# RMSNorm with swish: 32-row groups per partition for loads and stores, and a small transfer ahead of gamma's

## The chip, the cores and the metric

The kernel runs on one core of a Trainium2 chip. The metric is the device time of an execution in microseconds (us); the kernel before has a median of 160.43 us over 12 runs (160.1 to 160.9). A profile is one execution recorded by the hardware profiler. Its span runs from the first to the last recorded work of the program, and the device time is a little longer. The names in it: DVE is VectorE, ACT is ScalarE, POOL is GpSimd, SP is SyncE, whose only work here is to issue loads and to wait. "ACTq" and "SPq" are the sequencers that issue transfers. TensorE has no work in this kernel.

## The reference

The input is 16 x 1024 rows of 512 float32 values; every row is treated alone.

```python
rms = np.sqrt(np.mean(x ** 2, axis=-1, keepdims=True) + eps)
x_norm = x / rms * gamma
return (x_norm * (1.0 / (1.0 + np.exp(-x_norm)))).astype(np.float32)
```

That is 33.55 MB in and 33.55 MB out. A row is 2 KB.

## The kernel before

**Tiles.** The 16384 rows are cut into eleven tiles, one after the other in HBM. Tile `t` takes `sizes[t]` rows for each of the 128 partitions: 4, 4, 8, then six times 16, then 8 and 8, which makes 128 rows per partition. Within a tile, partition p holds consecutive rows, so for a tile of 16 rows each partition moves one contiguous piece of 32 KB, and the whole tile is contiguous in HBM. The buffer `xb` has room for 96 rows per partition and is used as a ring: tile 0 to 7 fill it once, tiles 8, 9 and 10 use the places of tiles 0 to 3 again. Everything happens in place: rows are loaded into `xb`, normalised there, passed through swish there and stored from there.

**Chunks.** The work goes by chunks of 4 rows per partition, 32 in all. For chunk k:

- `square(k)` on ScalarE: the fourth row is squared with its sum accumulated (L159), the other three are squared into a PSUM buffer (L166). Before the first chunk of a tile, ScalarE waits for the tile's load.
- `sums(k)` on VectorE (L204): the three sums of squares from PSUM.
- GpSimd adds eps (L141) and takes the power -0.5 (L148).
- `norm(k)` on VectorE (L215): four instructions, one for each row, multiply by the reciprocal root and by gamma.
- `swish(k)` on ScalarE (L178), over all four rows.

**Order.** The order on each engine is written out by hand. VectorE runs sums(k) and then norm(k-1). ScalarE runs square(k), then any store that is due, then swish(k-2). A store of a tile (L183) is issued from ScalarE's queue two chunks after the tile's last chunk number, so that it does not hold up the queue; it waits for the last swish of its tile. The PSUM buffer exists twice, so square(k) also waits for sums(k-2).

**Transfers.** Loads are issued by SP in order (L118), as early as the ring lets them: tiles 0 and 1 even ahead of the program's starting barrier, tiles 2 to 7 right after it; tile 8 waits for the stores of tiles 0, 1 and 2, tile 9 for that of tile 3 (L116). Gamma is loaded from ScalarE's queue into four partitions (L187) after GpSimd has zeroed the buffer (L136), and VectorE spreads it over the partitions (L228). At the end SP waits for all stores (L238).

Of the kernel before, what the change touches and what calls it, by code (L numbers as in the profile page):

```python
# [8 lines left out]
@with_exitstack  # L9
def kernel(  # L10
    ctx: ExitStack,
    tc: tile.TileContext,
    x: bass.AP,
    gamma: bass.AP,
    eps: bass.AP,
    out: bass.AP,
):
    nc = tc.nc
    P = nc.NUM_PARTITIONS
    AF = mybir.ActivationFunctionType  # L20
    ALU = mybir.AluOpType
    fp32 = mybir.dt.float32
    bf16 = mybir.dt.bfloat16

    xf = x.flatten_outer_dims()
    of = out.flatten_outer_dims()
    R, D = xf.shape


    sizes = [4, 4, 8] + [16] * 6 + [8, 8]  # L30
    ring = 96
    early = 2
    cn = 4
    n_sq = 3
    N = sum(sizes)
    assert N * P == R, (N, R)


    tiles = []
    done = 0  # L40
    for sz in sizes:
        assert done % ring + sz <= ring
        tiles.append((done * P, sz, done % ring))
        done += sz
    T = len(tiles)

    chunks = [
        (t, r, r == at)
        for t, (_, sz, at) in enumerate(tiles)
        for r in range(at, at + sz, cn)  # L50
    ]
    K = len(chunks)
    ends = []
    e = 0
    for sz in sizes:
        e += sz // cn
        ends.append(e)

    inv_d = 1.0 / float(D)
    eps_f = float(eps)  # L60

    tc.close()
    tc.compile()  # L65

    def sbuf(name, shape, dt=fp32):
        return nc.alloc_sbuf_tensor(name, shape, dt).ap()

    xb = sbuf("xb", [P, ring, D])  # L70
    gamma4 = sbuf("gamma4", [P, D])
    gamma_sb = sbuf("gamma_sb", [P, D])
    junk = [sbuf(f"junk{i}", [P, D], bf16) for i in range(2)]
    neg_half = sbuf("neg_half", [P, cn])
    ms = sbuf("ms", [P, K, cn])
    aeps = sbuf("aeps", [P, K, cn])
    rstd = sbuf("rstd", [P, K, cn])
    sq = [nc.alloc_psum_tensor(f"sq{i}", [P, 4, D], fp32).ap() for i in range(2)]

    ld = [nc.alloc_semaphore(f"ld{t}") for t in range(T)]  # L80
    st = [nc.alloc_semaphore(f"st{t}") for t in range(T)]
    s_gld = nc.alloc_semaphore("s_gld")
    s_zero = nc.alloc_semaphore("s_zero")
    s_half = nc.alloc_semaphore("s_half")
    s_gamma = nc.alloc_semaphore("s_gamma")
    s_acc = nc.alloc_semaphore("s_acc")
    s_sq = nc.alloc_semaphore("s_sq")
    s_sum = nc.alloc_semaphore("s_sum")
    s_eps = nc.alloc_semaphore("s_eps")
    s_rstd = nc.alloc_semaphore("s_rstd")  # L90
    s_norm = nc.alloc_semaphore("s_norm")
    s_swish = nc.alloc_semaphore("s_swish")

    def need(ins, sem, value):
        return ins.wait_op(sem, value, "sem-ge")

    def dram(ap, t):
        first, sz, _ = tiles[t]
        return ap[first : first + P * sz].rearrange("(p n) d -> p n d", n=sz)

    def buf(t):
        _, sz, at = tiles[t]
        return xb[:, at : at + sz, :]


    stored_by_sync = set()

    def load(t):
        _, sz, at = tiles[t]
        waits = [  # L110
            u for u in range(t)
            if tiles[u][2] < at + sz and at < tiles[u][2] + tiles[u][1]
            and u not in stored_by_sync
        ]
        for u in waits:
            nc.sync.wait_ge(st[u], 16)  # L116
            stored_by_sync.add(u)
        return nc.sync.dma_start(out=buf(t), in_=dram(xf, t)).then_inc(ld[t], 16)  # L118

    entry = nc.main_func.blocks[0].instructions  # L120
    here = nc.cur_bb.bb.instructions
    for t in range(early):
        ins = load(t).ins
        assert here[-1] is ins or here[-1].name == ins.name
        here.pop()
        at = next(
            i for i, other in enumerate(entry)
            if other.engine == mybir.EngineType.SP
            and isinstance(other, mybir.InstDrain)
        )  # L130
        entry.insert(at, ins)
    for t in range(early, T):
        load(t)


    nc.gpsimd.memset(gamma4, 0.0).then_inc(s_zero, 1)  # L136
    nc.gpsimd.memset(neg_half, -0.5).then_inc(s_half, 1)  # L137
    nc.gpsimd.wait_ge(s_half, 1)
    for k in range(K):
        need(  # L140
            nc.gpsimd.tensor_scalar(  # L141
                out=aeps[:, k, :], in0=ms[:, k, :], scalar1=eps_f, scalar2=None,
                op0=ALU.add,
            ),
            s_sum, k + 1,
        ).then_inc(s_eps, 1)
        need(
            nc.gpsimd.tensor_tensor(  # L148
                out=rstd[:, k, :], in0=aeps[:, k, :], in1=neg_half, op=ALU.pow
            ),  # L150
            s_eps, k + 1,
        ).then_inc(s_rstd, 1)


    def square(k):
        t, at, first = chunks[k]
        if first:
            nc.scalar.wait_ge(ld[t], 16)  # L158
        acc = nc.scalar.activation(  # L159
            out=junk[k % 2], in_=xb[:, at + n_sq, :], func=AF.Square,  # L160
            scale=inv_d**0.5, accum_out=ms[:, k, n_sq : n_sq + 1],
        )
        if k >= 2:
            need(acc, s_acc, k - 1)
        acc.then_inc(s_acc, 1)
        square = nc.scalar.activation(  # L166
            out=sq[k % 2][:, 0:n_sq, :], in_=xb[:, at : at + n_sq, :],
            func=AF.Square, scale=inv_d**0.5,
        )
        if k >= 2:  # L170
            need(square, s_sum, k - 1)
        square.then_inc(s_sq, 1)

    def swish(k):
        _, at, _ = chunks[k]
        rows = xb[:, at : at + cn, :]
        need(
            nc.scalar.activation(out=rows, in_=rows, func=AF.Silu), s_norm, k + 1  # L178
        ).then_inc(s_swish, 1)

    def store(t):
        need(
            nc.scalar.dma_start(out=dram(of, t), in_=buf(t)), s_swish, ends[t]  # L183
        ).then_inc(st[t], 16)

    need(
        nc.scalar.dma_start(out=gamma4[0:P:32, :], in_=gamma.partition_broadcast(4)),  # L187
        s_zero, 1,
    ).then_inc(s_gld, 16)
    nc.scalar.preload_act_table_set("silu_and_others")  # L190
    stored = 0
    for k in range(K + 3):
        if k < K:
            square(k)
        while stored < T and ends[stored] <= k - 2:
            store(stored)
            stored += 1
        if 2 <= k < K + 2:
            swish(k - 2)


    def sums(k):
        need(
            nc.vector.tensor_reduce(  # L204
                out=ms[:, k, 0:n_sq], in_=sq[k % 2][:, 0:n_sq, :], op=ALU.add,
                axis=mybir.AxisListType.X,
            ),
            s_sq, k + 1,
        ).then_inc(s_sum, 1)

    def norm(k):
        _, at, _ = chunks[k]
        for j in range(cn):
            row = xb[:, at + j, :]
            ins = nc.vector.scalar_tensor_tensor(  # L215
                out=row, in0=row, scalar=rstd[:, k, j : j + 1], in1=gamma_sb,
                op0=ALU.mult, op1=ALU.mult,
            )
            if j == 0:
                need(ins, s_rstd, k + 1)  # L220
        ins.then_inc(s_norm, 1)

    for k in range(K + 1):
        if k < K:
            sums(k)
        if k == 0:
            need(
                nc.vector.stream_shuffle(gamma_sb, gamma4, [0] * 32), s_gld, 16  # L228
            ).then_inc(s_gamma, 1)
        if k == 1:  # L230
            nc.vector.wait_ge(s_gamma, 1)
        if k >= 1:
            norm(k - 1)


    for t in range(T):
        if t not in stored_by_sync:
            nc.sync.wait_ge(st[t], 16)  # L238

# [34 lines left out]
```

## Time and profile before

| what | value |
|---|---|
| median of 12 runs | 160.43 us (160.1 to 160.9) |
| the profiled execution's own time | 160.66 us |
| its span | 159.3 us |
| VectorE busy | 139.1 us, 87% of the span |
| ScalarE busy | 125.1 us, 79% |
| GpSimd busy | 83.4 us, 52% |
| moved by DMA | 67.14 MB, 421 GB/s over the span |
| DMA queues | q1 (SP, loads) 33.56 MB, q10 (ScalarE, stores and gamma) 33.56 MB |
| norm (L215) | 128 instructions, 87.7 us, 755 ns each |
| sums (L204) | 32 instructions, 56.4 us, 1761 ns each |
| swish (L178) | 32 instructions, 61.1 us, 1908 ns each |
| square into PSUM (L166) | 32 instructions, 45.9 us, 1433 ns each |

Times in a profile are counted from the span's start. The page shows the busy share of each engine in 40 equal slices, one digit for each in tenths; the row "DMA" is the mean of the 16 DMA engines. The chain is followed back from the last instruction: at every step to what released it. A row of the list of waits names who waited, for whom, the total, how often, and the longest. In the DMA view a queue's row has its packets, its megabytes and the share of the 16 engines' time.

### The profile page before, as it was taken

Reading aid. Unit: us, or ns where it says so; the run is one execution under the profiler, and the core shown is the slowest. Engines: PE = TensorE matmul, PEld = TensorE weight load, DVE = VectorE, ACT = ScalarE, POOL = GpSimd, SP = SyncE. Lnnn points to the kernel's source line nnn. Section 1 sums busy time; section 2 is a strip of 40 time slices with the busy share of each in tenths; the row PEclk is TensorE's granted clock in tenths of the full one; section 3 lists DMA queues with packets and bytes.
Section 4 is the critical chain, followed back from the end, with each engine's and each line's share of the span. In section 5 each row is a group of like instructions: output and inputs, shape, how many; then the busy total and the mean of one; then the engine's idle time right before and its main releaser. Section 6 shows DMA issues by size and latency. Waiting matters only on the chain.

```text
span 159.3 us, 437 instructions
## 1 busy us (share of the span) xinstructions
DVE 139.1 (87%) x162; ACT 125.1 (79%) x129; POOL 83.4 (52%) x70
## 2 busy tenths in 40 slices
DVE  0298977999999999999999999999999999996600
ACT  1939849888888889988888888888998888883410
POOL 1043552444455555444444445888888888889000
DMA  6999999989989999999999999899999999999995
GB/s 251 434 502 395 395 389 450 477 360 479 477 360 452 399 469 413 403 477 436 395 438 477 395 411 494 382 457 407 477 391 424 440 461 411 420 485 395 403 444 230
DMA packets 3179, 67.14 MB, mean 421 GB/s; under 512 B 356, under 2 KB 356, under 8 KB 360
## 3 DMA queue, kind: packets, MB, share of 16 engines
q1 hardware_dynamic: 1584, 33.56, 49.6%
q10 hardware_dynamic: 1592, 33.56, 49.0%
q14 instruction: 3, 0.02, 0.0%
HBM read 33.56 MB, written 33.55 MB: 421 GB/s over the span
## 4 chain that ended last, share of the span: by engine, by line
DVE 76%; DMA 13%; ACT 2%; POOL 2%; issue 0%; SPq 0%; ACTq 0%
DVE xb L215 47%; DVE ms L204 29%; DMA xb<-in_x_dram 13%; POOL aeps L141 2%; ACT xb L178 1%; ACT sq L166 1%; POOL rstd L148 1%; ACT junk L159 0%; SPq L118 0%; ACTq L158 0%
## 5 line engine op out<-in xcount | busy, mean ns | idle before, releaser
L215 DVE SCALAR_TENSOR_TENSOR xb<-xb,rstd,gamma_sb 128x512 f32<-128x512 f32 x128 | 87.7, 755 | 1.2 <-POOL rstd L148 1.2
L178 ACT ACTIVATE xb<-xb 128x2048 f32<-128x2048 f32 x32 | 61.1, 1908 | 17.6 <-DVE xb L215 17.6
L141 POOL TENSOR_SCALAR aeps<-ms 128x4 f32<-128x4 f32 x32 | 42.5, 1328 | 59.3 <-DVE ms L204 59.3
L204 DVE TENSOR_REDUCE ms<-sq 128x3 f32<-128x1536 f32 x32 | 56.4, 1761 | 9.5 <-ACT sq L166 9.5
L166 ACT ACTIVATE sq<-xb 128x1536 f32<-128x1536 f32 x32 | 45.9, 1433 | 0.0
L148 POOL TENSOR_TENSOR rstd<-aeps,neg_half 128x4 f32<-128x4 f32 x32 | 40.2, 1256 | 2.7
L159 ACT ACTIVATE junk<-xb 128x512 bf16<-128x512 f32 x32 | 19.7, 615 | 5.5 <-DMA xb<-in_x_dram 5.4
L159 ACT ACTIVATION_READ_ACCUMULATOR junk<-xb 128x1 f32 x32 | 6.0, 186 | 0.0
L190 ACT ACT_TABLE_LOAD x1 | 1.3, 1283 | 3.6 <-issue 3.6
L136 POOL MEMSET gamma<- 128x512 f32 x1 | 0.5, 524 | 1.5 <-POOLq L65 1.5
L228 DVE STREAM_SHUFFLE gamma_sb<-gamma 128x512 f32<-128x512 f32 x1 | 0.7, 718 | 0.0
L255 POOL MEMSET const-float32-0.0<- 128x1 f32 x1 | 0.1, 98 | 0.2 <-issue 0.2
L255 POOL MEMSET const-bfloat16-1.0<- 128x1 bf16 x1 | 0.1, 101 | 0.0
L255 POOL MEMSET const-uint8-127<- 128x1 uint8 x1 | 0.1, 101 | 0.0
L137 POOL MEMSET neg_half<- 128x4 f32 x1 | 0.1, 101 | 0.0
L255 POOL MEMSET const-float32-1.0<- 128x1 f32 x1 | 0.1, 98 | 0.0
L228 DVE LOAD_MASK_SELECT gamma_sb<-gamma x1 | 0.0, 15 | 0.0
## 6 DMA issues: line engine op xcount, KB each, us to landing
xb<-in_x_dram SPq DMA_DIRECT2D x6, 4096.0 KB, 44.5
out_dram<-xb ACTq DMA_DIRECT2D x6, 4096.0 KB, 30.1
xb<-in_x_dram SPq DMA_DIRECT2D x3, 2048.0 KB, 37.9
out_dram<-xb ACTq DMA_DIRECT2D x3, 2048.0 KB, 10.9
xb<-in_x_dram SPq DMA_DIRECT2D x2, 1024.0 KB, 5.7
out_dram<-xb ACTq DMA_DIRECT2D x2, 1024.0 KB, 19.7
gamma<-in_gamma_dram ACTq DMA_DIRECT2D x1, 8.0 KB
```

The source lines that it names most:

```text
L136: nc.gpsimd.memset(gamma4, 0.0).then_inc(s_zero, 1)
L137: nc.gpsimd.memset(neg_half, -0.5).then_inc(s_half, 1)
L141: nc.gpsimd.tensor_scalar(out=aeps[:, k, :], in0=ms[:, k, :], scalar1=eps_f, scalar2=None, op0=ALU.add,),
L148: nc.gpsimd.tensor_tensor(out=rstd[:, k, :], in0=aeps[:, k, :], in1=neg_half, op=ALU.pow),
L159: acc = nc.scalar.activation(out=junk[k % 2], in_=xb[:, at + n_sq, :], func=AF.Square, scale=inv_d**0.5, accum_out=ms[:, k, n_sq : n_sq + 1],)
L166: square = nc.scalar.activation(out=sq[k % 2][:, 0:n_sq, :], in_=xb[:, at : at + n_sq, :], func=AF.Square, scale=inv_d**0.5,)
L178: nc.scalar.activation(out=rows, in_=rows, func=AF.Silu), s_norm, k + 1
L190: nc.scalar.preload_act_table_set("silu_and_others")
L204: nc.vector.tensor_reduce(out=ms[:, k, 0:n_sq], in_=sq[k % 2][:, 0:n_sq, :], op=ALU.add, axis=mybir.AxisListType.X,),
L215: ins = nc.vector.scalar_tensor_tensor(out=row, in0=row, scalar=rstd[:, k, j : j + 1], in1=gamma_sb, op0=ALU.mult, op1=ALU.mult,)
L228: nc.vector.stream_shuffle(gamma_sb, gamma4, [0] * 32), s_gld, 16
L255: nc = _bacc.Bacc("TRN2", target_bir_lowering=False, num_devices=1)
```

## The change

Two things change; what is computed for a row does not.

First, a new tensor `scratch` in HBM and a new buffer `blank` in SBUF, both 128 x 16 float32 (8 KB). GpSimd sets `blank` to zero before its other memsets, and ScalarE's queue sends `blank` to `scratch` ahead of gamma's load. SP waits for that transfer after its last load.

Second, the rows are cut into four groups of 32 rows per partition. Within a group, partition p holds 32 consecutive rows (64 KB), and the ring is three groups, the same 96 rows. A load or a store moves a piece (group, first row, number of rows) of a group: for every partition some of its 32 rows, so neighbouring partitions lie 64 KB apart in HBM. The nine loads take 4, 4, 8 and 16 rows of group 0, all 32 rows of group 1 and of group 2, and 16, 8 and 8 rows of group 3. The eight stores take 16 and 16 rows of group 0, all 32 of group 1, 16 and 16 of group 2, and 16, 8 and 8 of group 3. A load into a place that was used before waits for the stores of the group three earlier that overlap it: load 6 for store 0, load 7 for store 1. Chunks and the order of work on each engine follow the same rules as before; `chunks` now names, for the first chunk of each load, the load to wait for.

```diff
-    sizes = [4, 4, 8] + [16] * 6 + [8, 8]
-    ring = 96
+    gn = 32
+    G = R // (P * gn)
+    assert G * P * gn == R, R
+    loads = [(0, 0, 4), (0, 4, 4), (0, 8, 8), (0, 16, 16)]
+    loads += [(g, 0, gn) for g in range(1, G - 1)]
+    loads += [(G - 1, 0, 16), (G - 1, 16, 8), (G - 1, 24, 8)]
+    stores = [(0, 0, 16), (0, 16, 16)]
+    stores += [(g, 0, gn) for g in range(1, G - 2)]
+    stores += [(G - 2, 0, 16), (G - 2, 16, 16)]
+    stores += [(G - 1, 0, 16), (G - 1, 16, 8), (G - 1, 24, 8)]
+    ring = 3
...
+    chunks = []
+    for i, (g, r, n) in enumerate(loads):
+        for c in range(r, r + n, cn):
+            chunks.append((g % ring * gn + c, i if c == r else None))
     K = len(chunks)
-    ends = []
-    e = 0
-    for sz in sizes:
-        e += sz // cn
-        ends.append(e)
+
+    ends = [(g * gn + r + n) // cn for g, r, n in stores]
...
+    scratch = nc.dram_tensor("scratch", [P, 16], fp32, kind="Internal").ap()
+    blank = sbuf("blank", [P, 16])
+    s_blank = nc.alloc_semaphore("s_blank")
+    s_scratch = nc.alloc_semaphore("s_scratch")
...
-    def dram(ap, t):
-        first, sz, _ = tiles[t]
-        return ap[first : first + P * sz].rearrange("(p n) d -> p n d", n=sz)
-
-    def buf(t):
-        _, sz, at = tiles[t]
-        return xb[:, at : at + sz, :]
+    def dram(ap, piece):
+        g, r, n = piece
+        rows = ap[g * P * gn : (g + 1) * P * gn]
+        return rows.rearrange("(p n) d -> p n d", n=gn)[:, r : r + n, :]
+
+    def buf(piece):
+        g, r, n = piece
+        at = g % ring * gn + r
+        return xb[:, at : at + n, :]
...
+    def load(i):
+        g, r, n = loads[i]
+        for u, (h, q, m) in enumerate(stores):
+            if h == g - ring and q < r + n and r < q + m and u not in stored_by_sync:
+                nc.sync.wait_ge(st[u], 16)
+                stored_by_sync.add(u)
+        return nc.sync.dma_start(
+            out=buf(loads[i]), in_=dram(xf, loads[i])
+        ).then_inc(ld[i], 16)
...
-    for t in range(early, T):
+    for t in range(early, len(loads)):
         load(t)
-
-
+    nc.sync.wait_ge(s_scratch, 16)
+
+
+    nc.gpsimd.memset(blank, 0.0).then_inc(s_blank, 1)
     nc.gpsimd.memset(gamma4, 0.0).then_inc(s_zero, 1)
...
+    need(nc.scalar.dma_start(out=scratch, in_=blank), s_blank, 1).then_inc(
+        s_scratch, 16
+    )
     need(
         nc.scalar.dma_start(out=gamma4[0:P:32, :], in_=gamma.partition_broadcast(4)),
         s_zero, 1,
...
-        while stored < T and ends[stored] <= k - 2:
+        while stored < len(stores) and ends[stored] <= k - 2:
             store(stored)
             stored += 1
```

## The prediction

> **What bounds the kernel now.** I read the page's busy times, slices and chain first.
>
> ```profile
> DVE 139.1 (87%) x162; ACT 125.1 (79%) x129; POOL 83.4 (52%) x70
> ...
> DMA  6999999989989999999999999899999999999995
> ...
> DVE 76%; DMA 13%; ACT 2%; POOL 2%; issue 0%; SPq 0%; ACTq 0%
> ```
>
> The chain lies 76% on VectorE and 13% on one load, yet the DMA engines are full in nearly every slice. Two limits almost coincide, so order matters more than totals. The chain in order of time shows where the first one starts:
>
> ```profile
> 2.27 20.52 DMA xb<-in_x_dram
> ...
> 24.97 1.76 DVE ms L204
> ...
> 42.32 1.67 DVE ms L204
> 43.99 2.65 DVE xb L215 x4
> ...
> 149.90 1.91 ACT xb L178
> ```
>
> Load 3 lands at 2.27+20.52 = 22.8. ScalarE squares chunk 4, and at 24.97 (2.15 later) VectorE starts it. From there it never idles until the last chunks: 1.67+2.65 = 4.32 us a chunk, chunk 8 at 42.32. So a wait in VectorE after 24.97 is not made up. The timeline around chunk 8 tells when its rows are needed:
>
> ```profile
> 39.86 0.61 ACT L159 ACTIVATE junk<-xb 128x512 bf16<-128x512 f32 x1
> 40.38 0.19 ACT L159 ACTIVATION_READ_ACCUMULATOR junk<-xb 128x1 f32 x1
> 40.47 1.43 ACT L166 ACTIVATE sq<-xb 128x1536 f32<-128x1536 f32 x1
> ```
>
> Squaring ends at 41.9 and VectorE takes it at 42.3. Rows of chunk 8 must land by about 40.2; in the kernel before, chunk 8 needs only 48 rows per partition landed (load 4), the rest comes later.
>
> How loads and stores share the engines is in the DMA view of 24 to 34 us (queue: packets, MB, share), where loads have 32 KB rows and stores 8 KB rows, and of 68 to 76 us, where both have 32 KB:
>
> ```profile
> q1 hardware_dynamic: 105, 3.44, 80.0%
> q10 hardware_dynamic: 103, 0.71, 16.9%
> ...
> q1 hardware_dynamic: 54, 1.77, 51.2%
> q10 hardware_dynamic: 51, 1.67, 48.3%
> ```
>
> q1 is SP's (loads), q10 ScalarE's (stores). Of the first 103, 16 are semaphore writes: about one row against one row, whatever its size. Bytes therefore go by row size. The total stays at some 432 GB/s (window 60 to 100).
>
> **What the Trainium skill says.** "DMA: Bandwidth & Descriptors", section "Queues, rings and completion order": each DMA engine takes turns between the queues with work, switching at packet boundaries. The counts agree, a row being the unit. The same page, "Why a DMA increments its semaphore by 16 and not by 1": the full count is reached only when every engine's part has landed; thus no row of a 32-row load may be used before all are there. It also says there that contiguous rows longer than 64 KiB have to be cut; I read that as 64 KB still being one packet. No run here shows it. The same page, "Anatomy of one DMA": about 2.0 us plus bytes/436 GB/s (fitted on another issue path). The last store's 7.5 us from issue to landing fits loosely: 2.0+4.8 = 6.8, and it was queued behind its predecessor. "Perfetto Trace Analysis", "DMA Optimizations": splitting lets parts start sooner; this change merges.
>
> **The change, part by part.**
>
> *Scratch transfer.* GpSimd gets one small memset (0.1 us, as neg_half's). ScalarE's queue gets one issue more, 0.34 us (a store's) to 1.09 us (gamma's), ahead of gamma's issue and the table load, which now runs 3.57 to 4.85. The first squares slip from 4.87 by as much; gamma's shuffle too. Cover: ScalarE's 3.0 us wait for load 2, which ends at 12.27, and then load 3. Without that cover, up to 1.1 us. On the DMA engines: 128 rows of 64 bytes, 8 an engine. Nearest row: gamma's 2 KB packets, 84 ns in the trace's DMA records, so at most 0.7 us, at least nothing; I take 0.2, and it does delay the loads, since they are back to back. If it takes a start-up cost off the first real store (whose neighbouring load packets ran 1.3 to 1.7 us instead of 1.21 near 18 to 20 us), up to 0.9 is gained; I take none. SP's added wait stands behind all loads, ahead only of its closing waits: nothing.
>
> *First group.* Its loads keep 4, 4, 8 and 16 rows, now with 64 KB from partition to partition in HBM. Row lengths and order are the same; I charge nothing (a bad address pattern would add to every load; no row shows one). Its stores were 4, 4, 8, 16 rows from 16.2 us on; now 16 and 16, the first issued after chunk 3's swish, the place of the third store before (31.35). So load 3 no longer shares: from load 2's landing at 12.2, 4.19 MB at 432 GB/s take 9.7, landing 21.9 instead of 22.8. Chunk 4 starts up to 0.9 earlier.
>
> *Load 4 becomes 32 rows, and that is the step that decides.* Chunk 8 now waits for 16.78 MB. From 12.2 (4.19 MB landed) the other 12.58 MB take 29.1: 41.3 at the earliest, without any store and already 1.1 after the 40.2 at which it is needed. The first store is issued near 30.7 (31.35 less some 0.7). The first store before was issued at 16.19 and its packets began at 20.3 (DMA records): 4.1 us, so about 34.8. Load 4's 64 KB packets take 2x1.21 = 2.42 us; started near 21.3, they end at 33.4, 35.8, 38.2, 40.6. The store enters at 35.8 and puts one 32 KB packet (1.21) before each of the last two: +2.4. Landing 41.3+0.2+2.4 = 43.9. Bounds: one packet (42.7) if 64 KB packets make the store wait longer, three (45.1) if it enters by 33.4; none, 41.5.
>
> Blocked behind that wait on ScalarE are the squares of chunk 8, swish of chunk 6, then the rest; VectorE finishes sums 7 and norm 6 and then stands at sums 8, with norm 7 behind it. Sums 8: 43.9+2.15 = 46.05, against 42.32: 3.7 later. Swish 7, hence the second store, slip equally, to 48.6+3.7 = 52.3.
>
> *Load 5, also 32 rows.* It follows load 4 at 43.5. Six packets of store 0 remain, then store 1's; each of load 5's eight goes with one of 32 KB: 8x3.63 = 29.0, landing about 73. Chunk 16 needs it at 40.2+8x4.32+3.7 = 78.5: 5 us to spare. Load 6 waits for store 0 (done near 65), loads 7 and 8 for store 1 (near 87); needed after 112, 129 and 138. The 64 KB store, issued near 83.1+3.7, takes four fifths of the bytes against their 16 KB rows, but both are in by about 130. No second wait; a short DMA gap near 88 costs nothing now, as the engines have become the looser limit.
>
> *Fewer issues* (9 loads for 11, 8 stores for 11): 0.34 us each on a sequencer that waits for norms anyway: nothing. Packet overhead: 0.611 us for 16 KB and 1.213 for 32 KB leave 9 ns a packet; 40 packets fewer per engine give 0.4 us of DMA time, off the path.
>
> *End.* Sums 8 to the last swish's end is unchanged: 151.81+3.7 = 155.5. The second-last store, issued at 143.55+3.7, is done near 154, so the last meets idle engines: 6.9 us (2.0+4.9) instead of 7.5. Span 162.4, against 159.3: +3.1. The profiled execution took 160.66, 1.36 around its span, and stands 0.23 above the median of 160.43. Forecast 160.43+3.1 = 163.5.
>
> **The rivals.**
>
> *One or no store packet ahead of load 4's end:* 162.3 or 161.1. For it: a queue that holds several packets already, when they are twice as large. Against: the 4.1 us seen. *Three packets:* 164.7, if the scratch transfer or the queue makes the store enter quickly.
>
> *64 KB rows are cut into two packets.* Then load 4 shares one for one with 32 KB: five pairs remain at 34.8, landing near 47.3, 3.4 later than forecast: 166.9. For it: no such row in the profile. Against: the reading of the skill above.
>
> *Not slower: load 4 is in time.* The place is chunk 8's squares. The tail gets 0.6 back, so the break-even landing is 40.8, i.e. 12.58 MB in 28.6 us, 440 GB/s with no store in between. If so the earlier chunk 4 counts and the end comes up to 0.9 earlier: 159.5. For it: longer rows have less overhead. Against: 9 ns of 1213 is under 1%, and the first store is issued 10 us before.
>
> *The change only reshuffles* (a landing of 41.0 or so, loss and gain cancel): 160.4.
>
> **How the numbers follow.** Two packets 0.46, three 0.20, one or none 0.18, cut rows or bad addresses 0.09, cancelled 0.04, in time 0.03. The range 161.6 to 165.8 holds two, three and most of one, with 0.3 to 1 us for scratch, addresses and the tail. A measurement of this kernel can tell about 0.2%, 0.3 us. Slower by more 0.92, within 0.05, faster 0.03.
>
> **What would show it.** Right: ScalarE's wait at its first square for a load that lands near 44, longest about 4 to 5 us; VectorE idle by about as much before sums 8, and no wait at chunk 16; chunk 4 near 24.2; between 36 and 43 us the loads with twice the stores' bytes; DMA slices below 9 near 140 and 155; the last store at about 155.5, landing in about 7 us. Wrong: load 4 landed by 41 (rate or sharing misjudged), packets of 32 KB in q1 (cut rows), a VectorE wait at chunk 16 or later, loads 0 to 3 later than 4.7, 7.2, 12.2 and 22 (addresses or scratch).

## The result

The changed kernel takes 165.31 us (median of 8 runs, 165.03 to 165.81), the kernel before 160.31 (32 runs). The ratio is 1.031, 95% interval 1.0296 to 1.0325: slower by 5.0 us. The forecast was 163.5 with a range of 161.6 to 165.8. Ratios leave out executions more than 1.5% above the fastest of the same kernel, which matters in one experiment only.

The span of the profiled execution is 163.9 us, before it was 159.3. The page of the changed kernel, busy times and slices, and the chain's shares:

```profile
DVE 139.1 (85%) x162; ACT 125.2 (76%) x129; POOL 91.7 (56%) x71
...
DVE  0249999999129999999999999999999999999600
...
DMA  7999999599998997999999989999799997699947
...
DVE 63%; DMA 26%; ACT 2%; POOL 2%; SPq 0%; issue 0%; ACTq 0%
```

VectorE's row of the kernel before:

```profile
DVE  0298977999999999999999999999999999996600
```

VectorE does the same 139.1 us of work, but has a hole in slices 10 and 11, counted from 0 (41 to 49 us), which the row before did not have. The DMA row, full nearly throughout before, now shows unused time at 135 to 143 us (76% in use, 95% before) and at 154 to 158 us (48%, 91% before): the limit has moved. The 5 in slice 7 is no such gap: a packet is counted whole in one place, and the window of 28 to 32 us has 121%. The chain in order of time (start, duration, what) says what fills the hole:

```profile
2.75 43.05 DMA xb<-in_x_dram
...
47.98 1.76 DVE ms L210
...
155.67 1.91 ACT xb L180
```

The load on the chain is no longer load 3, landing at 22.80, but load 4, landing at 45.80. The sums of chunk 8 start at 47.98; before, they started at 42.32. The list of waits (who waited for whom, total, times, longest) has both ends of it:

```profile
DVE ms L210 <- ACT sq L168: 13.3, 2, 7.0
ACT junk L161 <- DMA xb<-in_x_dram: 9.7, 3, 6.5
```

Before, they were:

```profile
DVE ms L204 <- ACT sq L166: 9.5, 3, 7.0
ACT junk L159 <- DMA xb<-in_x_dram: 5.4, 3, 3.0
```

7.0 of VectorE's 13.3 is the first chunk's start; the other 6.3 is chunk 8. ScalarE waited 6.5 for the load. From there the chunks follow each other at 4.32 us to the last.

### The profile page after: what moved, and what is told of

Same layout as the page of the kernel before. It is cut to its first block, busy times and chain, and to the rows that moved or that the text cites. A ratio compares the mean times of both kernels' runs of the same rounds, so it can differ in the third digit from the quotient of the medians.

```text
span 163.9 us, 431 instructions
## 1 busy us (share of the span) xinstructions
DVE 139.1 (85%) x162; ACT 125.2 (76%) x129; POOL 91.7 (56%) x71
## 4 chain that ended last, share of the span: by engine, by line
DVE 63%; DMA 26%; ACT 2%; POOL 2%; SPq 0%; issue 0%; ACTq 0%
DVE xb L221 39%; DMA xb<-in_x_dram 26%; DVE ms L210 24%; POOL aeps L143 2%; ACT xb L180 1%; ACT sq L168 1%; POOL rstd L150 1%; SPq L116 0%; ACT junk L161 0%; ACTq L160 0%
## 5 line engine op out<-in xcount | busy, mean ns | idle before, releaser
L143 POOL TENSOR_SCALAR aeps<-ms 128x4 f32<-128x4 f32 x32 | 52.4, 1639 | 56.8 <-DVE ms L210 56.8
L210 DVE TENSOR_REDUCE ms<-sq 128x3 f32<-128x1536 f32 x32 | 56.6, 1768 | 13.3 <-ACT sq L168 13.3
L150 POOL TENSOR_TENSOR rstd<-aeps,neg_half 128x4 f32<-128x4 f32 x32 | 38.4, 1201 | 2.7
```

What stands on the lines that cost most here:

```text
L143: nc.gpsimd.tensor_scalar(out=aeps[:, k, :], in0=ms[:, k, :], scalar1=eps_f, scalar2=None, op0=ALU.add,),
L150: nc.gpsimd.tensor_tensor(out=rstd[:, k, :], in0=aeps[:, k, :], in1=neg_half, op=ALU.pow),
L210: nc.vector.tensor_reduce(out=ms[:, k, 0:n_sq], in_=sq[k % 2][:, 0:n_sq, :], op=ALU.add, axis=mybir.AxisListType.X,),
```

## The experiments

Each run is the changed kernel with the edit shown, unless said otherwise; times are medians, ratios are to the kernel before on the same chip.

**No store in load 4's way.** Store 0 is issued two chunks later.

```diff
-        while stored < len(stores) and ends[stored] <= k - 2:
+        while stored < len(stores) and ends[stored] <= k - 2 and (stored or k >= 8):
```

> The changed kernel with store 0 issued only after the squares of chunk 8, so that no store can stand in load 4's way. Theory (load 4's landing sets the time; 41.3 us by its bytes, plus about 1 us as the first store starts, plus a store row before each of its last two rows and before its completion write, 1.2 us each): load 4 lands at 41.2 to 41.8, sums 8 start near 43.6, the span is about 159.6 and the time about 161.0. Rival (64 KB rows, or rows 64 KB apart, are themselves slow): load 4 still lands after 44 and the time stays above 163.5.

The chain and VectorE's timeline of this run:

```profile
2.75 38.47 DMA xb<-in_x_dram
```

```profile
43.40 1.76 DVE L210 TENSOR_REDUCE ms<-sq 128x3 f32<-128x1536 f32 x1 [0.56 <-ACT sq L168]
```

Load 4 lands at 41.22 and the sums of chunk 8 start at 43.40, as the theory had it: 64 KB rows that lie 64 KB apart load at the full rate (12.58 MB from load 2's landing at 12.03, 431 GB/s), and all of the 4.6 us beyond 41.2 in the changed kernel came with the store. But the time is 164.01 (1.0219, 1.0184 to 1.0254), 3 us above what was expected. The gain was given back at the end. Transfers were now late instead: chunk 30 waited 1.2 us for load 8, which landed at 137.4, and the last store, issued at 152.91, took 9.9 us to land instead of 6.3, because the engines still had stores queued. Its completions came in between 159.0 and 162.8.

**The same bytes in thin rows.** Store 0 is cut into four stores of 4 rows, all issued at the same place.

```diff
-    stores = [(0, 0, 16), (0, 16, 16)]
+    stores = [(0, r, 4) for r in range(0, 16, 4)] + [(0, 16, 16)]
...
-    ends = [(g * gn + r + n) // cn for g, r, n in stores]
+    ends = [4] * 4 + [(g * gn + r + n) // cn for g, r, n in stores[4:]]
```

> The changed kernel with store 0 cut into four stores of 4 rows (8 KB rows), all issued at the place of store 0. The bytes waiting are the same. Theory that a row takes turns with a row: three rows of 0.31 us stand ahead of load 4's end instead of three of 1.21, so it lands near 43.1 and the time is about 162.6. Rival (the engines divide by bytes or by time): it lands near 45.8 as before, 165.3.

The chain of this run:

```profile
2.75 39.88 DMA xb<-in_x_dram
```

Load 4 lands at 42.63, 3.2 earlier than with 32 KB rows, although as many store bytes were waiting. Turns go by rows. The time is 163.83 (1.0212, 1.0178 to 1.0246), 1.2 above what was expected: half of the 3.2 is missing again, and again it is the last store, issued 3.2 earlier (154.41) and landing only 1.5 earlier (162.38).

In the changed kernel the turns can be counted. Its DMA view of 36 to 43 us (queue: packets, MB, share):

```profile
q1 hardware_dynamic: 32, 2.10, 69.1%
q10 hardware_dynamic: 32, 1.05, 34.7%
```

Two load rows of 64 KB and two store rows of 32 KB on each of the 16 engines: a row is one packet, they take turns one for one, and the loads get two thirds of the bytes. And the view of 44 to 45.4 us:

```profile
q10 hardware_dynamic: 19, 0.62, 102.9%
q1 hardware_dynamic: 16, 0.00, 0.6%
```

Load 4's data is through by 44.1; what q1 still sends is 16 packets without bytes to speak of, the completion writes, one an engine. They fall among store rows: in the DMA records each engine's write stands 1.2 us after the end of its last load row, with one store row of 1.213 us between them. With store 0 late, where no store row was waiting, it stands within 0.01 us. So the completion write waits for its turn as well, behind a third store row.

**Load 4 alone in two halves.**

```diff
-    loads += [(g, 0, gn) for g in range(1, G - 1)]
+    loads += [(1, 0, 16), (1, 16, 16)]
+    loads += [(g, 0, gn) for g in range(2, G - 1)]
```

> The changed kernel with load 4 alone cut into two loads of 16 rows (load 5 stays whole). Theory: no wait at chunk 8, its 16 rows land near 31.5; but load 5's eight 64 KB rows now each go with a 32 KB store row from about 47 us, landing near 77.5, and chunk 16 needs it at about 74: the wait moves there, some 3 us, time 162.3 to 163.3. Rival (only the first large load is late, load 5 has 5 us to spare as in the changed kernel): no wait anywhere, 159.8 to 160.5.

VectorE's timeline of this run, its one wait after the first chunks:

```profile
79.74 1.76 DVE L211 TENSOR_REDUCE ms<-sq 128x3 f32<-128x1536 f32 x1 [2.66 <-ACT sq L169]
```

The wait moved to chunk 16 and load 5, which landed at 77.56; the time is 162.52 (1.014, 1.0096 to 1.0184). Load 5's room in the changed kernel existed only because chunk 8 had already been late.

**Without the scratch transfer** (its buffer, memset, issue and waits removed).

```diff
-    nc.sync.wait_ge(s_scratch, 16)
...
-    nc.gpsimd.memset(blank, 0.0).then_inc(s_blank, 1)
...
-    need(nc.scalar.dma_start(out=scratch, in_=blank), s_blank, 1).then_inc(
-        s_scratch, 16
-    )
```

> The changed kernel without the scratch transfer, its buffer, memset and waits. Theory (it is hidden): gamma lands about 2 us earlier, load 4 lands within 0.3 of 45.8, the time stays at 165.3 within 0.4. Rival one (it prepares the write path for the first store): load 4 lands 0.5 or more later, time 165.8 and up. Rival two (its 128 packets cost the loads time): load 4 lands 0.3 to 0.7 earlier, time 164.6 to 165.0.

The chain:

```profile
2.75 42.99 DMA xb<-in_x_dram
```

Load 4 lands at 45.74 against 45.81: the transfer neither delays the loads nor prepares the stores. The four times fell apart, though: 163.8, 163.9, 165.3 and 165.4 (1.0256, 1.0197 to 1.0315). Two experiments below are about that.

**The scratch transfer alone**, added to the kernel before in the same way (its buffer and SP's wait are not shown).

```diff
+    nc.gpsimd.memset(blank, 0.0).then_inc(s_blank, 1)
     nc.gpsimd.memset(gamma4, 0.0).then_inc(s_zero, 1)
...
+    need(nc.scalar.dma_start(out=scratch, in_=blank), s_blank, 1).then_inc(
+        s_scratch, 16
+    )
```

> The kernel before with the scratch transfer added ahead of gamma's and nothing else. Theory (hidden): gamma lands 2 to 3 us later, covered by VectorE's 1.9 us wait before chunk 4 but for some tenths, time within 0.4 of before. Rival one (it warms the store path): the loads beside the first store no longer run slow, 0.3 to 0.6 faster. Rival two (128 packets in the loads' way): 0.5 or more slower.

Its waits:

```profile
DVE ms L213 <- ACT sq L172: 7.4, 2, 7.0
...
DVE gamma_sb L237 <- DMA gamma<-in_gamma_dram: 2.1, 1, 2.1
```

160.14 us, ratio 0.999 (0.9972 to 1.0009): no difference. Gamma landed at 10.9 instead of 8.5 and VectorE waited 2.1 for it, but the wait before chunk 4 shrank from 1.9 to 0.4. It is hidden, and only just: gamma's arrival varies, and in other profiled executions with the scratch transfer it came as late as 12.0 (store 0 late) and chunk 4 began at 25.5, against 25.0 in the kernel before.

**Both large loads in halves.**

```diff
-    loads += [(g, 0, gn) for g in range(1, G - 1)]
+    loads += [(g, r, 16) for g in range(1, G - 1) for r in (0, 16)]
```

> The changed kernel with both large loads, 4 and 5, cut into loads of 16 rows; the store of 64 KB rows stays. Theory (the waits for 64 KB loads are all that costs time on VectorE): no wait on VectorE after chunk 4, last store issued near 151.5; then the DMA engines set the end, and as they drift apart after the 64 KB store (3.8 us between first and last engine's end in the run with store 0 late) the time is 160.3 to 161.5. Rival (the 64 KB pitch or the scratch transfer costs time besides): above 161.8.

Nine of twenty executions took 160.3 to 161.3 us, within the theory's range, and eleven 162.8 to 164.4, within the rival's; the median of all is 162.8. The ratio, 1.0009 (0.9993 to 1.0026), is that of the nine alone, so this version by itself does not decide between the two. All that it has and the next version has not is the 64 KB store, and the next has no execution above 161.5. That the store brings the longer executions is likely but not shown: the one execution with a trace is of the nine. In it there was no wait at chunk 8 or 16; chunk 30, against the expectation, waited 1.7 us for the last load.

**Every row at most 32 KB**: the edit above, and the one store of 64 KB rows in two.

```diff
-    stores += [(g, 0, gn) for g in range(1, G - 2)]
+    stores += [(g, r, 16) for g in range(1, G - 2) for r in (0, 16)]
```

> The changed kernel with every load and store cut to at most 16 rows (32 KB): what is left of the change is the 64 KB pitch, the later first stores and the scratch transfer. Theory (row length is the whole cost): within 0.4 of the kernel before, 159.8 to 160.6, last store landing within 1.5 us on all engines. Rival (pitch, late first stores or scratch cost something): above 160.8.

160.6 us in 14 runs (160.4 to 161.5), ratio 1.001 (0.9996 to 1.0024). With the pitch of 64 KB, the later first stores and the scratch transfer all still there, the slowdown is gone. The pieces of 32 rows are the cause. For load 4 it is not the length of its rows as such: by the turns counted above, two rows of 64 KB let two store rows pass, where four of 32 KB would let four. It is that chunk 8 has to wait for all 32 rows at once. VectorE still has a wait here, for the last load at chunk 30:

```profile
139.94 1.76 DVE L210 TENSOR_REDUCE ms<-sq 128x3 f32<-128x1536 f32 x1 [3.19 <-ACT sq L168]
```

The time is that of the kernel before all the same, because here the transfers set the end, as they did there.

**Store 0 late, and the 64 KB store in two**: the edit of the first experiment and the store edit just shown.

> The run with store 0 late, and its one store of 64 KB rows cut into two of 32 KB. Theory (64 KB store rows pull the engines apart): the last store's landings lie within 1.5 us instead of 3.8, time 161.0 to 162.3. Rival (the late start of the stores alone makes the end late): still 163.5 to 164.3.

161.72 us (1.0076, 1.0057 to 1.0096), 2.3 less than with store 0 late alone. So the 64 KB store held back that run's end: the load that chunk 30 had waited for until 137.4 now landed at 126.8. That it pulls the engines apart is half shown: the last store's completions lay 2.2 us apart, less than 3.8, more than the 1.5 expected; and in the profiled execution with both loads halved they lay 1.1 apart with the 64 KB store in place.

**The 64 KB store in two, alone.** Only the store edit.

> The changed kernel with its one store of 64 KB rows cut into two stores of 16 rows. Theory (only load 4's landing matters, the DMA engines have slack after it): same as the changed kernel within 0.5, load 4 landing at 45.8. Rival (the 64 KB store costs something of the 5 us): 0.7 or more faster.

164.69 us (1.0261, 1.0214 to 1.0307; runs from 163.1 to 165.5), load 4 landing at 45.84. Against the spread of the changed kernel in the next run, four runs tell no difference, though the one of 163.1 lies below every run of it. In the profiled executions this store made none: the last store was issued at 157.62 and landed at 163.89, against 157.60 and 163.88 with the 64 KB store.

**The changed kernel again.**

> The changed kernel itself, once more, to see how its times spread. In its profile GpSimd's add took 0.66 us up to chunk 15 and 2.65 from chunk 16 on, and the last norm waited 1.24 us for it; without the scratch transfer the profiled run kept 0.66 to the end and the four times were 163.8, 163.9, 165.3 and 165.4. Theory A (that step happens in some executions and not in others, whatever the scratch transfer): times in two clusters near 163.9 and 165.3. Theory B (the scratch transfer brings it): all near 165.3.

163.9, 164.0, 164.0, 165.3, 165.6 and 165.8 us (1.0279, 1.0241 to 1.0318): two clusters, the scratch transfer present in all, so theory B is out. The first set of 8 runs, all at 165.0 to 165.8, lay in the upper one; why all of it did isn't known.

That GpSimd's step (its add going from 0.66 to 2.65 us) makes the clusters, as theory A has it, can be seen only where there is a trace. The profiled execution of 163.82 without the scratch transfer had no step, and its last norms followed without a wait:

```profile
148.84 5.37 DVE L212 SCALAR_TENSOR_TENSOR xb<-xb,rstd,gamma_sb 128x512 f32<-128x512 f32 x8
```

Its last store was issued at 156.18 and landed at 162.47, 1.4 before the changed kernel's at 157.60 and 163.88, although load 4 had landed within 0.1 of the same time. The profiled executions at 165.2 and 165.8 of the changed kernel, and at 165.3 with the 64 KB store in two, had the step and the wait. One traced execution of the lower cluster is little, but its end comes 1.4 us earlier, which is what lies between the clusters.

**Without GpSimd's add.** This kernel leaves out eps: the power is taken of the mean square. (The add, which stands above these lines, is removed.)

```diff
-                out=rstd[:, k, :], in0=aeps[:, k, :], in1=neg_half, op=ALU.pow
+                out=rstd[:, k, :], in0=ms[:, k, :], in1=neg_half, op=ALU.pow
             ),
-            s_eps, k + 1,
+            s_sum, k + 1,
```

> The changed kernel with GpSimd's add of eps left out, so that the power is taken of the mean square itself. Theory (in the changed kernel's last chunk the norm waits 1.24 us for GpSimd, since nothing else covers it there): no wait at the last norm, the last store 1.2 to 1.4 us earlier, time 163.7 to 164.1 in one cluster. Rival (the end is set by the transfers): 165.3 as before.

VectorE's timeline at the last norm, in the changed kernel and in this one:

```profile
152.90 2.74 DVE L221 SCALAR_TENSOR_TENSOR xb<-xb,rstd,gamma_sb 128x512 f32<-128x512 f32 x4 [1.24 <-POOL rstd L150]
```

```profile
152.56 2.74 DVE L214 SCALAR_TENSOR_TENSOR xb<-xb,rstd,gamma_sb 128x512 f32<-128x512 f32 x4 [0.90 <-POOL rstd L143]
```

The forecast missed. Four of five runs stayed at 164.9 to 165.2, one took 164.1 (1.028, 1.0258 to 1.0303). In this run the power went from 1.45 to 3.44 us at chunk 23; in the changed kernel's profile it was the add, from 0.66 to 2.65 at chunk 16. The 2.0 us fall on the operation that comes first after GpSimd's wait, which in both versions is also the one that reads VectorE's sums; these two readings are not told apart. Removing the add only passed them on. That the last norm's wait is exposed in the changed kernel is seen: with a wait 0.34 shorter, the last store was issued 0.33 earlier (157.27) and landed 0.33 earlier (163.55). Removing the wait altogether wasn't achieved.

## Why the prediction was right, and where its sizes were off

**The deciding step, load 4, was right in kind and short by 1.9 us.** Forecast landing 43.9, measured 45.81, outside the prediction's own bounds for it, 41.5 to 45.1. Its terms:

| term | forecast | measured |
|---|---|---|
| bytes alone | 41.3 | 41.22 (store 0 late) |
| scratch transfer | 0.2 | 0 (45.74 without, 45.81 with) |
| two store rows before the last two load rows | 2.4 | 2.4 (2 and 2 packets an engine, 36 to 43 us) |
| first store's start | 0 | 0.98 |
| a store row before the completion write | 0 | 1.21 |
| landing | 43.9 | 45.81 |

The measured terms add to 41.22+2.42+0.98+1.21 = 45.83. That this is only 0.02 off is chance: with store 0 late, the load rows ran 0.24 us an engine longer between 30 and 41 us without any store, so the first term is good to some 0.2. The first store was issued at 30.75 (forecast near 30.7); its rows began at 36.4 to 36.9, in the gap foreseen, though 5.7 us after the issue and not 4.1. The two terms at zero are the error. For the start, the prediction named the slow load packets of the kernel before but counted them only as a possible gain: it assumed that the scratch transfer could take the cost away and else that nothing changed. In the changed kernel's DMA records the load packet then in flight on each engine took 3.3 to 3.6 us instead of 2.42, 15.6 us over the 16 engines, 0.98 each. For the completion write, the text noted that semaphore writes count as packets, and then did not let this one take its turn. With thin rows the same sum gives 41.22 + 0.66 (that run's lengthening) + three rows of 0.31 = 42.81, measured 42.63.

**Chunk 4 earlier, and worth nothing:** 24.37 (forecast near 24.2), load 3 at 21.76 (21.9). But it was no longer load 3 that set it. VectorE's timeline of the changed kernel:

```profile
10.83 0.01 DVE L234 LOAD_MASK_SELECT gamma_sb<-gamma  x1 [2.08 <-DMA gamma<-in_gamma_dram]
...
24.37 1.75 DVE L210 TENSOR_REDUCE ms<-sq 128x3 f32<-128x1536 f32 x1
```

Behind the scratch transfer gamma landed at 10.80 instead of 8.52, 2.3 later where the prediction had reckoned with up to 1.1, and from there VectorE ran without a wait to chunk 8. Without the scratch transfer chunk 4 began at 23.78, after a wait of 1.00 for its load. The wait at chunk 8 covered the difference.

**From sums 8 to the end** the slip was handed on whole, as forecast: 47.98 - 42.32 = 5.66 at chunk 8, and 157.60 - 151.84 = 5.76 at the last store's issue. Forecast was 3.7; ScalarE's wait for load 4 was 6.5 instead of 4 to 5.

**The tail** was overpriced: 6.3 us from issue to landing on idle engines, forecast 6.9 with the fixed part of 2.0 us that the Trainium skill gives in "DMA: Bandwidth & Descriptors", "Anatomy of one DMA", for another issue path. The changed kernel's last store:

```profile
DMA to landing us min/median/max: 6.3/6.3/6.3
```

The 2 MB take 4.9 at 0.611 us a row, so some 1.4 is fixed, and for this path the measured 1.4 is the figure to use. Of 5.76, 1.2 thus came back (7.5 to 6.3, forecast 0.6), and the span grew by 4.6 instead of 3.1. The medians are 5.0 apart: the profiled execution of the kernel before took 0.35 more than its median of 160.31, that of the changed kernel 0.07 less.

**Load 5 and the rest** landed at 75.4 (forecast about 73), 91.2, 110.4 and 129.6 (needed after 112, 129 and 138), without a wait. The experiment with load 4 in halves shows that the "5 us to spare" was borrowed from chunk 8's delay.

**Rivals.** Of the forecast's cases "three packets" (164.7) came nearest, and in effect three rows did stand in the way, though the third was ahead of the completion write and not of data. Cut rows are ruled out: the view of 36 to 43 us has 65.5 KB a packet in q1. The prediction had inferred that a 64 KB row is one packet from a sentence on longer rows that does not say so; these packets show it. A load in time was never near: even alone it landed at 41.22, after the 40.8 of break-even.

**How much was luck.** The wait, its place and its cause were as forecast. That the time also fell into the range, 0.5 below its upper end, is in part luck: the landing lay beyond the three-packet case, and the tail gave back 0.6 more than was counted on.

**What stays open.** The changed kernel's clusters at 163.9 and 165.4 go with GpSimd's 2 us step in the few executions that have a trace; its trigger no run shows. Part of the 5.0 us lies there: the 1.24 us wait of the last norm was present before as well, but there the transfers were the later ones at the end and covered most of it. The kernel before with the scratch transfer had no step in its profile and issued its last store 1.34 earlier, at 150.50, but that landed only 0.5 earlier, at 158.80. The forecast took over the end of the kernel before with this wait in it, so it is to be held against the upper cluster; that 163.5 lies near the lower one is chance.

No version here beats the kernel before. Its DMA engines are in use without a gap from 2 to 156 us (431 GB/s); the versions that removed the waits came back to that limit, not below it.

## What to carry to other kernels

A transfer is usable only when its last byte and its completion are in, so merging loads moves the first use to the end of the whole (here from 31.5 us, the landing of load 4's first 16 rows as a load of their own, to 45.8): compare that landing, bytes over rate plus what can get between, with the moment at which the first rows are wanted. Loads and stores that meet on the DMA engines share by rows, so the row length sets who gets the bytes. When engine and transfers are almost equally limiting, a gain on one side shows only up to the other's limit: two of these versions gained 3.2 and 4.6 us at chunk 8 and kept 1.5 and 1.3 against the changed kernel's 165.3, and nothing against the lower of its clusters.

## What the runs showed that was not expected

- A completion write takes its turn like a row: one store row of 1.21 us stood before it.
- The first store into an idle store queue lengthens the load packets then in flight: by 0.49 us an engine in all with 8 KB store rows in the kernel before (beside 32 KB load rows), 0.66 with 8 KB and 0.98 with 32 KB store rows beside 64 KB load rows. With 32 KB store rows beside 32 KB load rows it was 0.93 to 1.15 (load 4 or both large loads in halves, every row at most 32 KB), so it goes by the store's rows more than by the load's. A small store issued long before did not take this away.
- From some chunk on, in some executions, GpSimd's first operation after a wait takes 2.0 us more (0.66 to 2.65, or 1.45 to 3.44), and the power after it 0.35 less (1.39 to 1.04). Seven of the thirteen profiled executions have it, that of the kernel before from chunk 21 on. With both large loads in halves it ended again at chunk 30, behind VectorE's wait there. It costs nothing while VectorE has other work; at the last chunk VectorE waited 0.9 to 1.2 us for it.
- A 64 KB row is one packet of 2.418 us, twice the 1.213 of 32 KB but for 8 ns, and rows 64 KB apart in HBM load as fast as contiguous ones (loads 0 to 2 at 4.7, 7.2 and 12.1 us, in the kernel before at 4.7, 7.2 and 12.2).
